# The last features of the second feed-forward product, token by token in the slab scheme's banks

## The chip, the cores and the metric

The kernel runs on one core of one Trainium2 chip. The metric is the device time of one execution in microseconds; 1983.56 us is the median of three runs before the change (1983.42 to 1984.15). Matrix products run on TensorE (PE, its weight loads as PEld), elementwise work on VectorE (DVE) and ScalarE (ACT); GpSimd (POOL) and SyncE (SP) issue transfers.

## What is computed

The reference is a two-layer decoder trunk over 256 tokens of 2048 features, in float32. Layer 0 mixes tokens with a multi-scale causal pooling and a memory cross-attention; layer 1 with a differential attention over shared keys and values and the memory attention. Each layer ends in the same feed-forward block, which is all that matters here:

```python
def squared_relu_mlp(h, w1, w2):
    z = jax.nn.relu(h @ w1)
    return (z * z) @ w2
...
        x = x + squared_relu_mlp(rms_norm(x, ffn_norm[i]), w_ff1[i], w_ff2[i])
```

`w_ff1` is 2048 x 8192 and `w_ff2` 8192 x 2048. The norm's per-token factor is applied after the second product, since relu and the square let it through: as `r[0]` (features by tokens) or `r[1]` (one scalar per token row).

## The kernel before

**Precision.** Every product is made of three matmuls. A 128 x 128 weight block is cast to a high part (ACT, line 195, into `hi_ring`) and a low part is the difference (DVE, line 198, into `lo_ring`); activations are held as high and low too. High times low, high times high and low times high are accumulated in PSUM.

**Feed.** `Feed` streams the weights in the order of use: it loads (SP, `load`), prepares (`_prepare`, `_split`) and hands out blocks. A dry run of the program lists the jobs in order of use; `Plan.close` turns that into the order of preparation. The two rings have `SLOTS = 6` slots of 512 columns. When a job is asked for (`fill`), up to three further entries are prepared if slots are free. Jobs of kind `N` are four blocks for plain use (a quad, one slot); jobs of kind `S` belong to slabs. The casts and low parts of `S` jobs are bound to their order by `feed.order`; the framework's planner orders the rest by its own estimates.

**Slabs.** A slab takes two features (128 rows each of `w_ff2`) and eight blocks of columns for all 256 tokens in the seven products of a Strassen-Winograd scheme instead of eight. Each product has its PSUM bank `banks[0]` to `banks[6]`, which accumulates over slabs. A slab is run in four jobs (lines 943, 945 and 946 are the three matmuls of a product): job 0 uses banks 0 and 1 with plain weights, job 1 bank 2, job 2 banks 3 and 4, job 3 banks 6 and 5 with sums of weights. The sums are made like this, for slab n, with `ra` the first loaded row of blocks and `rb` the second: after job 0's split, POOL adds a part of the second row into `ra` while it is loaded (line 170); the entry `K`, ahead of job 1, adds on DVE (line 224) `ra` and `rb`; job 1 uses the left half of `ra`; job 2 uses `rb`; after job 2's split POOL adds the same part into `rb` (line 170) and DVE adds `ra`'s right half (line 238); job 3 uses `rb`. So

```python
        if p[2] == 0:
            self.add_right(p[1], ra[:, 0:512])
        elif p[2] == 2:
            self.add_right(p[1], rb[:, 512:1024])
            add(rb[:, 0:512], rb[:, 0:512], ra[:, 512:1024])
```

**The feed-forward block (`ffn`).** Of the first product, 8 of 64 output features go through eight slabs, and the other 56 through plain tiles (`up_tile`: 16 blocks each, lines 456 and 458, bank `x_bank`). After each tile its result is added, rectified, squared into `stage`, split into `z` (`convert`) and combined in pairs into sums of activations `sit`. The second product's slabs run between the blocks of the up-tiles: `jobs` is a list of due times (`tiles_at`, in units of up-tiles) in the order (n+1, 0), (n, 1), (n, 2), (n-1, 3). The 2048 outputs are two halves, g = 1 (the left one) and g = 0, which share the seven banks: `slabs` alternates in groups of four, and `swap` copies the banks out (line 1101) and back (line 1093) between them. The left half takes 24 slabs, the right half all 32. When the left half's last slab is done, `close_left` combines its banks, `scale_rows` scales them and `turn_left` transposes them into `resid`.

**The tail.** `last` runs after the 56 up-tiles. Twelve slab jobs are left by then, for the right half. The left half's last 16 features (pairs 24 to 31 hold 16 features; the right half's are done by slabs) are done in eight plain `down_tile`s, one for each of the left half's output blocks, each with 16 blocks; two slab jobs stand ahead of each of the first six. `finish_banks` closes the right half during tile 5. In layer 1 the last tile is made of finer matmuls (`c_tile`, lines 470 to 472), its last four features from `zr`, already scaled. `done(n)` hands a finished output on: to the next layer's operand in layer 0, to the output in layer 1 (line 2049).

Of the kernel before, what the change touches and what calls it, by code (L numbers as in the profile page):

```python
# [17 lines left out]
P = 128  # L18
# [8 lines left out]
PER_PART = 56  # L27
# [28 lines left out]
class Plan:  # L56
# [7 lines left out]
    def __init__(self):  # L64
        self.entries = []
        self.npos = 0
        self.jobs = []
        self.slabs = []

# [31 lines left out]
class Feed:  # L101
# [65 lines left out]
    def add_right(self, n, t):  # L167

        h = self.plan.row["S", n, 1]
        self.nc.gpsimd.dma_start(t, self.wst[h, :, 0:512], accum_op=ALU.add)  # L170
# [40 lines left out]
    def _prepare(self, p):  # L211
# [22 lines left out]
        if p[2] == 0:  # L234
            self.add_right(p[1], ra[:, 0:512])
        elif p[2] == 2:
            self.add_right(p[1], rb[:, 512:1024])
            add(rb[:, 0:512], rb[:, 0:512], ra[:, 512:1024])
# [35 lines left out]

    def used(self, n=1):
# [6 lines left out]
    def slab(self, rows):  # L282

        if self.dry:
            self.plan.slabs.append(rows)
        self.slab_no += 1
# [10 lines left out]
    def job_used(self, n, j):  # L297
        if not self.dry:
            self.free(("S", n, j))

# [11 lines left out]
def program(ctx, tc, plan, dry, xT, memT, par, lam, cst, wst, yT):  # L312
# [129 lines left out]
    def a_part(ps, w, l, n, ks, xs, first=True, last=True, between=None, rows=None):  # L442
# [4 lines left out]
        while i < len(ks):  # L447
# [7 lines left out]
            for c, k, hi, lo in two:  # L455
                nc.tensor.matmul(ps, hi, xs[:, k, :], start=first and c == 0, stop=False)  # L456
# [337 lines left out]
    def ffn(l, xs, tags, done, z, sums_in, f_place):  # L794
# [6 lines left out]

        room = sp.tile([P, 8192], F32, tag=tags[1], name=f"room{l}")
        staged = sp.tile([P, 2048], F32, tag="big2", name=f"stage{l}")
        sit = [sums_in[:, j, :] for j in range(4)]
        stage = [staged[:, T * j : T * j + T] for j in range(6)]
        sums = [room[:, 512 * j : 512 * j + 512] for j in range(2)]
        outs = [room[:, 1024 + 512 * j : 1536 + 512 * j] for j in range(2)]
# [19 lines left out]
        def evict(ps):  # L827
            x = outs[cnt[0] % 2]
            cnt[0] += 1
            return x, nc.scalar.copy(x, ps)  # L830
# [4 lines left out]
        def convert(j):  # L835
            a = stage[j % 6]
            k = j % NK

            def high():
                z_free[k] = False  # L840
                nc.scalar.copy(z[:, k, 0:T], a)
                at(1, low)

            def low():
                nc.vector.tensor_sub(z[:, k, T : 2 * T], a, z[:, k, 0:T].bitcast(F32))
# [3 lines left out]
            if j % 2 == 0:  # L849
                return  # L850
            i = j // 2

            def ready():
                return j in z_done and j - 1 in z_done and sit_free[i % 4]

            def combine():
                summed_up.add(i)
                sit_free[i % 4] = False
                a11, a21 = stage[2 * i % 6][:, 0:P], stage[2 * i % 6][:, P:T]
                a12, a22 = stage[(2 * i + 1) % 6][:, 0:P], stage[(2 * i + 1) % 6][:, P:T]  # L860
                s1, s2, s3, s4 = (sums[i % 2][:, c * P : c * P + P] for c in range(4))
                nc.vector.tensor_sub(s1, a21, a22)
                nc.vector.tensor_sub(s3, a11, a21)
                nc.vector.tensor_sub(s2, s1, a11)
                nc.vector.tensor_add(s4, a12, s2)
                at(1, sums_high)
                at(2, sums_low)

            def sums_high():
                nc.scalar.copy(sit[i % 4][:, 0:512], sums[i % 2])  # L870

            def sums_low():
                nc.vector.tensor_sub(
                    sit[i % 4][:, 512:1024], sums[i % 2], sit[i % 4][:, 0:512].bitcast(F32)
                )
                sit_done.add(i)

            when(ready, combine)

        def up_tile(i, ps, between=None):  # L880
# [5 lines left out]
            y, out = evict(ps)  # L886
            at(1, lambda: nc.vector.tensor_add(y[:, 0:T], y[:, 0:T], y[:, T : 2 * T]))
            at(2, lambda: nc.scalar.activation(y[:, 0:T], y[:, 0:T], AF.Relu))

            def square():  # L890
# [1243 lines left out]
```

## Time and profile before

| | |
|---|---|
| median of the runs | 1983.56 us |
| profiled execution | span 1982.8 us, 31946 instructions |
| TensorE, VectorE, ScalarE, GpSimd busy | 1977.6, 1806.6, 1571.6, 239.3 us |
| layer 0's feed-forward block | first up-tile at 252.2 us, plain down-tiles from 862.2 to 921 us |
| layer 1's | first up-tile at 1310.2 us, plain down-tiles from 1920.5 us to the end |
| transferred | 426.92 MB, mean 215 GB/s |

The page gives busy times of the engines, the span in 40 slices, the queues and the chain of work that ended last. Below it, the trace answers by groups of instructions, by stretches of time (busy microseconds of each engine), by tile or line (durations as min/median/max), and by the timeline (start, duration, engine, line, operation, output <- inputs). Times are from the span's start.

### The profile page before, as it was taken

What the parts mean: (1) busy time and instruction counts of PE and PEld (TensorE: products, weight loads), DVE (VectorE), ACT (ScalarE), POOL (GpSimd) and SP (SyncE); (2) the same over time, 40 slices, a digit from 0 to 9 for tenths busy, and PEclk for the clock granted to TensorE, in tenths of its full rate; (3) what the DMA queues carried; (4) which work ended last, traced back from release to release, by engine and by line L of the source; (5) the groups of instructions that cost most, each with busy time, mean ns of one, the idle gap of its engine ahead of it and who ended that gap; (6) DMA issues with size and microseconds to landing.
All of it is one profiled execution on the core that took longest, in us unless ns stands there. A gap on an engine that the chain in (4) does not pass through costs nothing.

```text
span 1982.8 us, 31946 instructions
## 1 busy us (share of the span) xinstructions
PE 1977.6 (100%) x10356; PEld 1685.5 (85%) x10356; DVE 1806.6 (91%) x3313; ACT 1571.6 (79%) x2886; POOL 239.3 (12%) x281
## 2 busy tenths in 40 slices
PE   9999999999999999999999999999999999999999
PEld 7888888888888888888888889888888888888888
DVE  8898889999999999889989798989999999999888
ACT  7766677788878888778768799777788888888775
POOL 0000011111111111110110000001111111111110
PEclk9999999999999999999999999999999999999999
DMA  9556578888888888767886434568888888988874
GB/s 312 183 183 195 189 207 229 236 232 235 237 233 232 231 233 227 226 182 222 246 222 191 166 127 143 197 188 240 235 231 229 235 234 229 242 231 227 227 207 146
DMA packets 151080, 426.92 MB, mean 215 GB/s; under 512 B 17024, under 2 KB 19712, under 8 KB 150912
## 3 DMA queue, kind: packets, MB, share of 16 engines
q1 hardware_dynamic: 111024, 352.50, 53.2%
q0 software_dynamic: 39744, 72.37, 22.0%
q8 instruction: 81, 1.33, 0.3%
q14 instruction: 87, 0.71, 0.1%
q10 hardware_dynamic: 144, 0.01, 0.0%
HBM read 422.72 MB, written 2.10 MB: 214 GB/s over the span
## 4 chain that ended last, share of the span: by engine, by line
PE 99%; DMA 0%; ACT 0%; SPq 0%; issue 0%; DVE 0%; ACTq 0%
PE x_bank L456 22%; PE x_bank L458 11%; PE p L943 10%; PE p L945 10%; PE p L946 10%; PE wo L456 6%; PE wo L458 3%; PE u L456 2%; PE ff L456 1%; PE u L458 1%; PE q L490 1%; PE q L492 1%; PE q L491 1%; PE mk L492 1%; PE mk L490 1%; PE vp L1642 1%
## 5 line engine op out<-in xcount | busy, mean ns | idle before, releaser
L195 ACT CAST hi_ring<-raw 128x512 fp32r<-128x512 f32 x897 | 547.5, 620 | 167.3 <-PE x_bank L456 39.7
L198 DVE TENSOR_TENSOR lo_ring<-raw,hi_ring 128x512 fp32r<-128x512 f32 x897 | 605.1, 686 | 46.7 <-ACT hi_ring L195 39.9
L456 PE MATMUL x_bank<-fx,hi_ring 128*128 128x512 f32 x1728 | 540.1, 394 | 0.0
L458 PEld LDWEIGHTS x_bank<-fx,lo_ring 128*128 128x128 f32 x1728 | 324.5, 188 | 73.5
L198 DVE TENSOR_TENSOR lo_ring<-room,hi_ring 128x1024 fp32r<-128x1024 f32 x256 | 312.7, 1222 | 44.1 <-ACT hi_ring L195 42.5
L195 ACT CAST hi_ring<-room 128x1024 fp32r<-128x1024 f32 x256 | 269.8, 1054 | 94.4 <-PE x_bank L456 43.2
L458 PE MATMUL x_bank<-fx,lo_ring 128*128 128x256 f32 x1728 | 339.6, 278 | 0.0
L456 PEld LDWEIGHTS x_bank<-fx,hi_ring 128*128 128x128 f32 x1728 | 286.3, 189 | 26.0 <-ACT room L830 1.5
L198 DVE TENSOR_TENSOR lo_ring<-slab,hi_ring 128x1024 fp32r<-128x1024 f32 (+1 forms) x276 | 263.3, 954 | 33.3 <-ACT hi_ring L195 30.2
L195 ACT CAST hi_ring<-slab 128x1024 fp32r<-128x1024 f32 (+1 forms) x276 | 227.7, 834 | 52.5 <-PE p L945 28.2
L170 POOL DMA_DIRECT2D slab<-in_w x138 | 119.6, 866 | 1172.0 <-DVE lo_ring L198 854.0
L943 PE MATMUL p<-hi_ring,sit 128*128 128x512 f32 x480 | 188.3, 392 | 0.0
L945 PE MATMUL p<-hi_ring,sit 128*128 128x512 f32 x480 | 187.4, 390 | 0.0
L946 PE MATMUL p<-lo_ring,sit 128*128 128x512 f32 x480 | 186.6, 389 | 0.0
L170 POOL DMA_DIRECT2D room<-in_w x128 | 110.8, 866 | 486.5 <-DVE lo_ring L198 456.6
L456 PE MATMUL wo<-cat,hi_ring 128*128 128x512 f32 x512 | 161.6, 397 | 0.0
L943 PE MATMUL p<-hi_ring,z 128*128 128x512 f32 x368 | 145.2, 395 | 0.1
L945 PE MATMUL p<-hi_ring,z 128*128 128x512 f32 x368 | 143.9, 391 | 0.0
L946 PE MATMUL p<-lo_ring,z 128*128 128x512 f32 x368 | 143.4, 390 | 0.0
L458 PEld LDWEIGHTS wo<-cat,lo_ring 128*128 128x128 f32 x512 | 95.9, 188 | 22.3
L946 PEld LDWEIGHTS p<-lo_ring,sit 128*128 128x128 f32 x480 | 90.1, 188 | 19.7
L943 PEld LDWEIGHTS p<-hi_ring,sit 128*128 128x128 f32 x480 | 90.0, 187 | 13.1
(495 smaller groups left out, 3610.7 us busy)
## 6 DMA issues: line engine op xcount, KB each, us to landing
raw<-in_w SPq DMA_DIRECT2D x446, 512.0 KB, 4.3
slab<-in_w SPq DMA_DIRECT2D x138, 512.0 KB, 5.7
slab<-in_w POOLq DMA_DIRECT2D x138, 256.0 KB, 5.3
room<-in_w SPq DMA_DIRECT2D x128, 256.0 KB, 4.7
room<-in_w POOLq DMA_DIRECT2D x128, 256.0 KB, 5.5
resid<-in_x SPq DMA_DIRECT2D x8, 256.0 KB, 5.1
kv<-in_mem SPq DMA_DIRECT2D x8, 256.0 KB, 5.3
out_y<-resid SPq DMA_DIRECT2D x16, 128.0 KB, 1.9
```

Source lines behind the costliest of these rows:

```text
L170: self.nc.gpsimd.dma_start(t, self.wst[h, :, 0:512], accum_op=ALU.add)
L195: self.last_cast = self.nc.scalar.copy(hi, src)
L198: low = self.nc.vector.tensor_sub(lo, src, hi.bitcast(F32))
L456: nc.tensor.matmul(ps, hi, xs[:, k, :], start=first and c == 0, stop=False)
L458: nc.tensor.matmul(ps[:, T : 2 * T], lo, xs[:, k, 0:T], start=False, stop=last and c == len(ks) - 1,)
L490: nc.tensor.matmul(ps[t], x[t][1], hi, start=k == 0, stop=False)
L491: nc.tensor.matmul(ps[t], x[t][0], hi, start=False, stop=False)
L492: nc.tensor.matmul(ps[t], x[t][0], lo, start=False, stop=k == NK - 1)
L943: nc.tensor.matmul(ps, a[1], hi, start=new, stop=False, **again)
L945: nc.tensor.matmul(ps, a[0], hi, start=False, stop=False, **again)
L946: nc.tensor.matmul(ps, a[0], lo, start=False, stop=end, **again)
L1642: nc.tensor.matmul(bank, a[0], lo, start=False, stop=end)
```

## The change

Both halves of the second product now go through the same slabs: 29 pairs of features in layer 0 (groups of 4, the last of 1: 58 slabs) and 30 in layer 1 (the last group of 2: 60 slabs). The three or two pairs left (`singles`) are done for both halves token by token: the activations of 128 tokens are the fixed operand and a quad of four weight blocks the moving one, and the result is added into banks 1 and 6 (first column group) or 4 and 2 (second), which hold plain outputs in the scheme (`plain_quad`). In layer 1 the right half's first column group is `held_quad`: all of bank 6 first, then all of bank 1, from the same four held quads.

`down_tile`, `finish_banks` and `zr` go. `last` becomes an explicit list: a quad or a slab job at a time, with layers 0 and 1 different. The right half is closed in steps (`close_right`, `close_c12`, `close_v`, `close_w`, `scaled_sum`, `turn`); its last piece in layer 1 is scaled in two halves, transposed and written out. `turn_left` adds from PSUM directly in layer 0 and through a POOL transfer in layer 1. The two features of a pair change places in the slab; a pair's second feature is split for one half of the tokens only (`Pairs` is the new layout of `z`), sums take three or one DVE operations in place of four, and in layer 1 (`BY_TWO`) two up-tiles are finished together. `far` is never set.

```diff
-PER_PART = 56
+GROUPS = ((4, 4, 4, 4, 4, 4, 4, 1), (4, 4, 4, 4, 4, 4, 4, 2))
+BY_TWO = (False, True)
...
         slabs = []
-        for h in range(6):
-            for g in (0, 1) if h % 2 == 0 else (1, 0):
-                slabs += [(g, 4 * h + i, g == h % 2) for i in range(4)]
-        slabs += [(0, i, False) for i in range(24, 32)]
+        for h, n in enumerate(groups):
+            first = sum(groups[:h])
+            g = (len(groups) - h) % 2
+            slabs += [(g, i, True) for i in range(first, first + n)]
+            slabs += [(1 - g, i, False) for i in range(first, first + n)]
+        n_slabs = len(slabs)
+        w = n_slabs - groups[-1] - 1
+        singles = range(left_pairs, 32)
...
-            return 12.5 + 0.78 * (p - 4) if p <= 47 else 46.04 + 1.6 * (p - 47)
+            if p <= 41:
+                return 12.5 + 0.78 * (p - 4)
+            return 41.36 + 14.2 * (p - 41) / (w - 42)
...
-        for p in range(-9, len(slabs) + 1):
+        for p in range(-9, w - 1):
...
+        def plain_quad(g, c, i, e):
+            hi, lo = feed.quad(weights(g, c, i, e))
+            for p in ((1, 6), (4, 2))[c]:
+                product(p, g, g == 0 and (i, e) == (31, 1), side(p, i, e), hi, lo)
+            feed.used(4)
...
         def last():
+            z_last = n_slabs - 1
+            plain(1, (0, 1), singles[:1])
+            slab((w - 1, 1), (w - 1, 2), (w - 2, 3))
+            if l == 0:
+                plain(1, (0,), singles[1:2])
+                slab((w - 1, 3))
+                plain(1, (1,), singles[1:2])
+                plain(1, (0, 1), singles[2:])
+                slab((w, 0), (w, 1), (w, 2))
+            else:
+                plain(1, (0, 1), singles[1:])
+                slab((w, 0), (w - 1, 3), (w, 1), (w, 2))
+            slab((w + 1, 0), (w, 3), (w + 1, 1), (w + 1, 2))
+            for s in range(w + 2, n_slabs):
+                slab((s, 0), (s - 1, 3), (s, 1), (s, 2))
+            if l == 0:
+                plain(0, (1,), singles[:1])
+                slab((z_last, 3))
+                plain(0, (0,), singles)
+                plain(0, (1,), singles[1:])
+            else:
+                plain(0, (1,), singles)
+                slab((z_last, 3))
+                for p in (6, 1):
+                    tail.extend(("held", p, i, e) for i in singles for e in range(2))
...
+                if x == ("held", 6, 31, 1):
+                    at(1, close_w)
+                if x == ("held", 1, 31, 0):
+                    turn(0, 1, "st")
+                if x == ("held", 1, 31, 1):
+                    for c in range(2):
+                        scaled_sum(1, right["c11"], 0, slice(T * c, T * c + T))
+                    turn(0, 0, "t", (0, 2))
+                    turn(0, 0, "t", (2, 4))
```

In this list `plain(g, cs, which)` stands for one quad for each of the named pairs, column groups and two features, and `slab((s, j), ...)` for job j of slab s. In layer 0 w is 56 and the slabs end at 57; in layer 1 w is 57 and they end at 59.

More of the change, by code (lines that the diff above doesn't have):

```diff
@@ L273, in block, with held, release @@
         return hi[:, s], lo[:, s]
+    def held(self, what):
+        both = self.quad(what)
+        self.pos += 4
+        if self.dry:
+            self.plan.npos = self.pos
+        return both, self.pos // 4 - 1
+    def release(self, n):
+        if not self.dry:
+            self.free(("N", n))
     def used(self, n=1):
@@ L859, in combine @@
[L859 to L866, printed above, removed]
+                summed_up.add(m)
@@ L1055, in close_first @@
             for p in of_job[j]:
-                restore(p, 0)
+                restore(p, slabs[0][0])
         def turn_first(h):
@@ L1271, in ffn @@
         due(56)
-        assert len(jobs) == 12 and not turns
         feed.loads_ahead = LOADS
-        ends = (
-            (2, 0, 0, 0), (2, 0, 0, 0), (2, 0, 0, 0), (2, 0, 0, 0), (2, 0, 0, 0), (2, 0, 0, 0),
-        )
         def last():
-            def some(n):
-                for _ in range(n):
-                    one_job()
-                    tick()
-            def between(n):
-                return lambda b: some(ends[n][b // 4]) if b > 0 and b % 4 == 0 else None
-            for n in range(8):
-                if n < 6:
-                    some(ends[n][0])
-                if n == 5:
-                    finish_banks()
-                ps = bank() if n < 6 else mmt("ff2")
-                down_tile(n, ps, between(n) if n < 6 else None)
+            z_last = n_slabs - 1
@@ new lines, in last, with slab, plain @@
+            tail = []
+            def slab(*what):
+                tail.extend(("slab", s, j) for s, j in what)
+            def plain(g, cs, which):
+                for i in which:
+                    tail.extend(("plain", g, c, i, e) for c in cs for e in range(2))
+            plain(1, (0, 1), singles[:1])
+            slab((w - 1, 1), (w - 1, 2), (w - 2, 3))
+            if l == 0:
+                plain(1, (0,), singles[1:2])
[3 more added lines that the diff above has]
+                slab((w, 0), (w, 1), (w, 2))
+            else:
+                plain(1, (0, 1), singles[1:])
+                slab((w, 0), (w - 1, 3), (w, 1), (w, 2))
@@ new lines, in can, with run @@
+            def can(what, *a):
+                if what == "slab":
+                    return ready(*a)
+                if what == "held":
+                    return holds[a[0]] == 0
+                g, c, i, e = a
+                if any(holds[p] != g for p in ((1, 6), (4, 2))[c]):
+                    return False
+                return i in sit_done if c else 2 * i + e in z_done
+            def run(what, *a):
+                if what == "slab":
+                    jobs[:] = [(0, *a)]
+                    one_job()
+                elif what == "held":
+                    held_quad(*a)
+                else:
+                    plain_quad(*a)
@@ L1296, in ffn @@
+            waited = 0
+            for x in tail:
+                while not can(*x):
+                    tick()
+                    waited += 1
+                    assert waited < 60, (l, x)
+                if turns:
+                    turn_left(turns.pop(0))
+                run(*x)
+                after(*x)
+                tick()
+            assert not turns
         return last
```

334 lines of the change are left out of this document (214 added, 120 removed).

## The prediction

> **What bounds the kernel now.** I read the page first: busy times, slices, and the chain that ended last.
>
> ```profile
> span 1982.8 us, 31946 instructions
> PE 1977.6 (100%) x10356; PEld 1685.5 (85%) x10356; DVE 1806.6 (91%) x3313; ACT 1571.6 (79%) x2886; POOL 239.3 (12%) x281
> PEclk9999999999999999999999999999999999999999
> PE 99%; DMA 0%; ACT 0%; SPq 0%; issue 0%; DVE 0%; ACTq 0%
> ```
>
> TensorE is busy from end to end at full granted clock and makes 99% of the last chain, so less matmul work shortens the run, and any wait that TensorE gains lengthens it one for one. The profiled execution (1982.8 us span) lies 0.8 us under the 1983.56 us median; I sum against the median.
>
> A busy row doesn't show the rate, because matmuls overlap. The timeline's start times do (slab products, then plain blocks of layer 1's tail, then the finer tiles and the transposes near the end):
>
> ```profile
> 1958.07 0.39 PE L945 MATMUL p<-hi_ring,z 128*128 128x512 f32 x1
> ...
> 1960.34 0.39 PE L946 MATMUL p<-lo_ring,sit 128*128 128x512 f32 x1
> 1960.57 0.62 PE L456 MATMUL x_bank<-z,hi_ring 128*128 128x512 f32 x2
> ...
> 1964.74 0.62 PE L456 MATMUL x_bank<-z,hi_ring 128*128 128x512 f32 x2
> ...
> 1973.18 0.28 PE L472 MATMUL ff<-z,lo_ring 128*128 128x256 f32 x1
> ...
> 1975.34 0.28 PE L472 MATMUL ff<-z,lo_ring 128*128 128x256 f32 x1
> ...
> 1975.46 0.27 PE L1185 MATMUL ct<-const,c_b 128*128 128x128 f32 x1
> ...
> 1976.22 0.27 PE L1185 MATMUL ct<-const,c_a 128*128 128x128 f32 x1
> ...
> 1979.08 0.28 PE L472 MATMUL ff<-zr,lo_ring 128*128 128x256 f32 x1
> 1979.39 0.42 DVE L915 TENSOR_TENSOR resid<-resid,ff 128x256 f32<-128x256 f32 x1 [0.55 <-PE ff L472]
> ```
>
> From 1958.07 to 1960.57 eleven 512-column matmuls start: 0.227 us each. So a slab job of two blocks (6 matmuls) is 1.36 us, job 1 (3 matmuls) 0.68, a slab (21) 4.77, and a token-by-token quad (6 matmuls, four blocks) 1.36. From 1960.57 to 1964.74 there are six pairs of plain blocks: 4.17/12 = 0.3475 us a block. In the last output tile six blocks take 2.16: 0.36 each. Eight transposes start 0.11 apart.
>
> **Matmul work removed.** Layer 0's plain part is 8 tiles of 16 blocks: 128 x 0.3475 = 44.5 us. In its place come two slabs (9.55) and 24 quads (3 pairs x 2 features x 2 halves x 2 column groups; 32.7): 42.3, a gain of 2.2. Layer 1 had the same 44.5, plus 16 x 0.0125 = 0.2 for its finer last tile; now four slabs (19.1) and 16 quads (21.8): 40.9, a gain of 3.8. Four of layer 1's last transposes move behind the last product: 0.4 less ahead of it. Together -6.4 us.
>
> **The end of layer 1.** Now the last matmul ends at 1979.36 and the span at 1982.8: 3.4 us, with one 0.42 us DVE operation and the output transfer. Afterwards the chain behind the last product is: two half-width scaled sums (0.42 each, the second overlapping), two transposes, a 0.42 add, then two more transposes, which reuse bank "t" and so wait for that add, a second add, and the transfer. By the rows above: 0.5 + 0.4 + 0.45 + 0.4 + 0.45 before a transfer of 2.95, so 5.1. Cost +1.7 (1.0 if the second pair overlaps, 2.5 if the strided output lands slower).
>
> **Main loops.** They take over two (layer 0) and three (layer 1) slabs from the tails, and two more swaps each of bank copies.
>
> ```profile
> 600.00:700.00 100.00, 100.00 (x509) 84.50 (x508) 93.31 (x146) 87.43 (x148) 18.73 (x22) 1.00 0.88 233
> 860.00:907.80 47.80, 47.80 (x258) 41.08 (x257) 43.75 (x76) 38.10 (x65) 3.46 (x4) 1.00 0.65 189
> L1101 ACT COPY room<-p x46: 570/585/599, 360.2 to 1743.4; 128x512 f32<-128x512 f32 x46
> ```
>
> Columns of the first two rows (busy by stretch): PE, PEld, DVE, ACT, POOL, clock, DMA share, GB/s. A swap is 14 ACT copies of about 0.59: 28 more, 16.5 us a layer, against 12.6 idle of each 100 us. The old schedule's pace is kept to slab 41; later slabs get 0.95 to 1.01 up-tiles where some had 0.78, so VectorE's 93% eases there; the merged sums and the halved conversion of the odd feature take work off it as well. I cost the main loops at nothing; the cover is ACT's and DVE's idle tenth, and without it a bank restore would arrive late. Layer 1's left half returns through a POOL transfer added into `resid`; the output transfers queued on SP behind it are needed by nobody before the end, and eight products follow. Nothing.
>
> **The wait that comes in.** Preparing a slab is a chain. After job 0's cast (ACT) and low part (DVE), POOL issues an accumulating transfer into the block that job 1 and the K sum read; after job 2's low part it issues a second one, into the block that job 3 reads. `feed.order` keeps slab casts and lows in that order. Before, the job order is (n+1,0), (n,1), (n,2), (n-1,3) with plain work between, so each accumulate has about a slab's period:
>
> ```profile
> 864.79 0.86 POOL L170 DMA_DIRECT2D room<-in_w  x1 [6.67 <-DVE lo_ring L198]
> 873.08 0.86 POOL L170 DMA_DIRECT2D slab<-in_w  x1 [7.43 <-DVE lo_ring L198]
> 880.71 0.86 POOL L170 DMA_DIRECT2D room<-in_w  x1 [6.76 <-DVE lo_ring L198]
> ...
> DMA to landing us min/median/max: 3.5/5.4/8.6
> ...
> DMA to landing us min/median/max: 2.6/3.8/5.5
> ```
>
> The last two rows are the landing times of all accumulates (line 170) and of the `room` transfers in layer 0's tail. In the new tails the order is (n,0), (n-1,3), (n,1), (n,2), with no quad between: slabs 56 and 57 of layer 0; 57, 58 and 59 of layer 1. Job 1's accumulate is then issued one preparation before it is needed, and job 3's likewise. The preparations cost:
>
> ```profile
> 866.21 1.22 DVE L198 TENSOR_TENSOR lo_ring<-room,hi_ring 128x1024 fp32r<-128x1024 f32 x1
> 867.34 0.68 DVE L873 TENSOR_TENSOR sit<-room,sit 128x512 fp32r<-128x512 f32 x1
> 867.94 1.29 DVE L198 TENSOR_TENSOR lo_ring<-raw,hi_ring 128x512 fp32r<-128x512 f32 x2
> ...
> L195 ACT CAST hi_ring<-room x7: 1034/1055/1060, 862.2 to 896.9; 128x1024 fp32r<-128x1024 f32 x7
> ```
>
> Start to start a 1024-wide DVE pass is 1.13 us and a 512-wide one 0.60. Follow one cycle, t = 0 when slab n's first accumulate lands. The accumulate for (n-1,3) landed 1.13 earlier; its cast ends at -0.08, its low at 1.05; the K sum ends at 1.65, job 1's low at 2.25, job 2's at 3.4, the next slab's job 0 at 4.6, its accumulate is issued at 4.9 and lands at 4.9 + L. TensorE has 4.77 us of products per slab, so each such cycle shows about L + 0.1. The ring of six slots holds 6 x 0.68 = 4.1 us of products and can hide this once, not per slab. Waits behind it: slab casts queue in order, so products of all later jobs are late too.
>
> Layer 0: the two slots of (56,0) come free as the last four quads start; cast, low and issue 2.6, L, and job 1's cast 0.6, against 4 x 1.36 + 1.36 = 6.8 of products: L - 3.6. Then one cycle, L + 0.1. Then (57,3) waits 0.3 + L + 1.05 against two quads and the rest of job 2, 3.4: L - 2.0. Layer 1: the first accumulate has four quads and two jobs, 8.2: nothing. Then two cycles, 2L + 0.2; (59,3) has four quads ahead: nothing. Together 5L - 5.3.
>
> The landing time L: bounds 3.5 (no accumulate was faster) and 8.6. A slab brings a 512 KB load, a 256 KB load and two 256 KB accumulates (their medians over all loads follow),
>
> ```profile
> slab<-in_w SPq DMA_DIRECT2D x138, 512.0 KB, 5.7
> slab<-in_w POOLq DMA_DIRECT2D x138, 256.0 KB, 5.3
> ```
>
> 1.31 MB in a cycle of over 9 us, some 140 GB/s and below the 189 of the tail's row. So the tail is nearest: 3.8 at the median, 5.5 at most. I take 4.5, a little above that median because the two accumulates now follow each other closely: 17 us; 12 at 3.5, 22 at the overall median 5.4. The adds and bank copies of `close_left` (7 x 0.60 on DVE, 9 x 0.59 on ACT) and job 2's add now stand in the same queues; if they go into the idle spells they cost nothing, if they block casts in program order each layer may lose their 4 to 9 us once. I take +1.
>
> Sum: 1983.56 - 6.4 + 1.7 + 17 + 1 = 1997 us.
>
> [...]
>
> **Rivals.** *Hidden, faster.* The waits don't reach TensorE at all, since preparation runs ahead. For it: no wait of TensorE shows in the tails today, and accumulates are not late anywhere. Against it: the ring's 4.1 us is spent once, and a cycle of 4.9 + L can't fit 4.77. Time: 1983.56 - 6.4 + 1.7 = 1979. It decides at a total wait of 4.7 us: below that the change gains, and below 0.7 it gains over 0.2%. Chance 0.2 (the casts' real order is set by a planner that I see only in its result).
>
> *Half hidden.* Only the full cycles show and L sits near its floor, or the planner finds work for the idle spells: 4 to 10 us of wait, 1983 to 1989. Chance 0.12.
>
> *Queues block.* The in-order casts also wait behind `close_left`'s copies, or L is at its overall median: 24 to 35 us of wait, 2003 to 2014. A cold clock would add to it:
>
> ```profile
> 1981.50:1982.00 0.50, 0.00 (x0) 0.00 (x0) 0.00 (x0) 0.00 (x0) 0.00 (x0) 1.00 0.00 0
> 1982.00:1982.50 0.50, 0.00 (x0) 0.00 (x0) 0.00 (x0) 0.00 (x0) 0.00 (x0) 0.59 0.00 0
> ```
>
> After the last matmul (1979.36) the granted clock falls within 3 us; five idle spells of 3 to 5 us could each be followed by about 3 us at half rate, 1.5 us lost each, 7 in all: 2004. [...] Chance of this rival 0.15.
>
> **How the numbers follow.** The forecast (1990 to 2003) has 0.53. A measurement here tells about 0.2%, 4 us, from no change. Faster (below 1979.6): most of *hidden*, 0.14. Same (to 1987.5): the rest of it and half of *half hidden*, 0.13. Slower 0.73. The range runs from the hidden case, 1979, to the upper part of *queues block*, 2012; the forecast's own range is 1990 to 2003.
>
> **What would show it.** Right: idle TensorE only in the two tails, 7 to 9 us each, ahead of slab products, with ACT casts of `slab` and `room` blocks waiting for DMA; the accumulates of the tails 1 us apart in pairs; last matmul to end 5.1 us; tails of TensorE work 2.2 and 3.8 us shorter when the waits are subtracted. Wrong: no DMA wait on ACT or DVE in the tails (then *hidden*), idle spells in the main loops (bank restores late, DVE short), a clock below 1.00 (cold), or landing times outside 3.5 to 5.5.

## The result and the profile after

The changed kernel is slower: 2004.33 us median of four runs (2003.05 to 2006.27) against 1983.80 (1983.42 to 1984.15) on the same chip, ratio 1.0105 (95% interval 1.0090 to 1.0119). That is inside the range (1979 to 2012), on the predicted side, and 7 us above the predicted 1997, just outside the forecast's own range of 1990 to 2003. The profiled execution is the longest of the four runs (2006.27, span 2004.4; the others' spans are 2001.2 to 2003.5), so its stages hold some 2 us that the median does not.

Span, busy times, the clock in 40 slices and the chain that ended last, from the page after:

```profile
span 2004.4 us, 31465 instructions
PE 1984.2 (99%) x10194; PEld 1674.8 (84%) x10194; DVE 1784.0 (89%) x3133; ACT 1572.1 (78%) x2831; POOL 253.0 (13%) x297
PEclk9999999999999999999999999999999999999999
issue 44%; PE 44%; POOL 9%; DMA 1%; DVE 1%; ACT 1%; POOLq 0%; SPq 0%; ACTq 0%; DVEq 0%
PE wo L496 6%; POOL slab L172 4%; POOL room L172 4%; PE x_bank L496 3%; PE wo L498 3%; PE p L997 2%; PE p L1000 2%; PE p L999 2%; PE u L496 2%; PE x_bank L498 2%; PE u L498 1%; PE q L530 1%; PE q L532 1%; PE q L531 1%; PE mk L530 1%
```

The chain is the first thing to read. Before, TensorE was 99% of it. Now the chain steps back from TensorE through a cast to a transfer and on to POOL's accumulating transfers (line 172, the old line 170): somewhere a wait for them ended last. From there back the chain stays on POOL through most of both main loops; its "issue" (44%) is mostly the time between POOL's transfers there, in which nothing is lost, so the shares of this chain aren't shares of the loss. The busy row does not show it: TensorE is still at 99%, with 162 matmuls fewer in the records and a busy time 6.6 us *longer*: a matmul's recorded duration grows behind a wait (0.50 us at 881.38 below, 0.39 at 879.59) and at half clock (0.63 at 903.15). Start times have to carry the ledger.

The span cut at start times of matmuls ("main" from the first to the last up-tile, "tail" from there to the next block's first key product, or in layer 1 to the last product; "middle" from that key product to layer 1's first up-tile; "end" from the last product's start to the end of the span), in us:

| kernel | start | main 0 | tail 0 | middle | main 1 | tail 1 | end | span |
|---|---|---|---|---|---|---|---|---|
| before | 252.2 | 607.8 | 60.7 | 389.5 | 608.1 | 60.8 | 3.7 | 1982.8 |
| after | 252.1 | 615.5 | 60.7 | 394.6 | 620.0 | 55.5 | 6.0 | 2004.4 |

The main loops take over two and three slabs (9.55 and 14.3) and give up 16 transposes of `turn_left` each (1.8): +7.8 and +12.5 worked out, +7.7 and +11.9 measured, so nothing waits there. A stretch of the main loop (columns as before: PE, PEld, DVE, ACT, POOL, clock, DMA share, GB/s) then some microseconds of the two tails, cut fine:

```profile
600.00:700.00 100.00, 100.00 (x508) 84.58 (x507) 92.73 (x141) 86.85 (x148) 18.60 (x22) 1.00 0.87 231
...
899.00:901.00 2.00, 0.14 (x1) 0.14 (x2) 1.36 (x3) 1.23 (x2) 0.28 (x1) 1.00 0.60 100
...
902.00:903.00 1.00, 1.00 (x3) 0.60 (x3) 0.85 (x3) 1.00 (x3) 0.00 (x0) 0.50 0.00 0
903.00:904.00 1.00, 1.00 (x4) 0.77 (x3) 1.00 (x2) 1.00 (x2) 0.00 (x0) 0.50 0.00 0
904.00:905.00 1.00, 1.00 (x3) 0.50 (x2) 0.77 (x2) 1.00 (x3) 0.00 (x0) 0.50 0.00 0
905.00:906.00 1.00, 1.00 (x6) 0.83 (x5) 1.00 (x2) 1.00 (x3) 0.07 (x1) 1.00 0.00 0
1965.00:1968.00 3.00, 1.01 (x5) 0.35 (x3) 1.77 (x4) 1.94 (x4) 0.86 (x1) 1.00 0.71 113
1968.00:1971.00 3.00, 2.45 (x8) 1.22 (x8) 2.77 (x4) 2.80 (x5) 0.00 (x0) 1.00 0.32 57
1976.00:1978.00 2.00, 0.79 (x5) 0.42 (x4) 0.00 (x0) 0.82 (x2) 1.40 (x2) 1.00 0.82 164
...
1980.00:1982.00 2.00, 2.00 (x8) 1.47 (x7) 1.34 (x2) 1.43 (x2) 0.86 (x1) 0.55 0.78 138
1982.00:1984.00 2.00, 2.00 (x7) 1.62 (x7) 1.73 (x2) 2.00 (x5) 0.21 (x1) 0.60 0.94 222
```

TensorE works 0.14 of 2 us, and then three or four matmuls a microsecond start where it should be 4.4: the granted clock is 0.50 for 3.4 us (901.6 to 905.0). ScalarE's own waits in the first tail (867 to 925 us) and in the second (from 1950 us), each as total, times, longest:

```profile
ACT hi_ring L197 <- DMA room<-in_w: 7.0, 3, 5.1
ACT hi_ring L197 <- DMA slab<-in_w: 5.2, 1, 5.2
...
ACT hi_ring L197 <- DMA slab<-in_w: 4.5, 2, 4.0
...
ACT hi_ring L197 <- DMA room<-in_w: 2.5, 3, 1.2
```

None of these waits for `slab` and `room` existed before. One of them in the timeline: POOL's accumulates, ScalarE's casts, and TensorE behind them (in brackets the idle time before, and what ended it):

```profile
874.44 0.86 POOL L172 DMA_DIRECT2D room<-in_w  x1 [13.42 <-DVE lo_ring L200]
889.00 0.87 POOL L172 DMA_DIRECT2D slab<-in_w  x1 [13.70 <-DVE lo_ring L200]
896.08 0.86 POOL L172 DMA_DIRECT2D room<-in_w  x1 [6.21 <-DVE lo_ring L200]
898.41 0.86 POOL L172 DMA_DIRECT2D slab<-in_w  x1 [1.47 <-DVE lo_ring L200]
...
880.29 1.04 ACT L197 CAST hi_ring<-room 128x1024 fp32r<-128x1024 f32 x1 [5.14 <-DMA room<-in_w]
...
892.69 0.62 ACT L197 CAST hi_ring<-slab 128x512 fp32r<-128x512 f32 x1 [5.24 <-DMA slab<-in_w]
899.77 1.04 ACT L197 CAST hi_ring<-room 128x1024 fp32r<-128x1024 f32 x1 [1.14 <-DMA room<-in_w]
...
879.59 0.39 PE L1000 MATMUL p<-lo_ring,z 128*128 128x512 f32 x1
881.38 0.50 PE L997 MATMUL p<-hi_ring,z 128*128 128x512 f32 x1 [1.40 <-ACT hi_ring L197]
...
900.86 0.50 PE L997 MATMUL p<-hi_ring,z 128*128 128x512 f32 x1 [1.87 <-ACT hi_ring L197]
```

The landing times of line 172's transfers in the two tails:

```profile
DMA to landing us min/median/max: 3.6/3.6/5.7
...
DMA to landing us min/median/max: 3.6/3.9/5.1
```

The accumulate issued at 896.08 lands 3.6 us later at 899.7; the cast starts at 899.77, the product at 900.86. To sum the waits, I take all matmuls that start over 0.26 us behind a 512-column one, and add up what lies beyond 0.227: 11.1 us in tail 0, 9.0 in tail 1, 8.2 in the middle (before: 0.2, 0 and 3.9). In tail 1 a further 1.7 us of idle time, ahead of 1978.39, stands behind a transpose and is not in its sum. The granted clock is 0.50 once in each of the three stages, for 3.4 us each time (901.6 to 905.0, 976.7 to 980.1, 1980.2 to 1983.6; never before the end of the work in the kernel before). Matmuls start 0.43 us apart there, so each of these stretches makes up to 1.7 us of its stage's sum.

### The profile page after: what moved, and what is told of

It reads as the page before. It is cut to its first block, busy times and chain, and to the rows that moved or that the text cites. A ratio compares the mean times of both kernels' runs of the same rounds, so it can differ in the third digit from the quotient of the medians.

```text
span 2004.4 us, 31465 instructions
## 1 busy us (share of the span) xinstructions
PE 1984.2 (99%) x10194; PEld 1674.8 (84%) x10194; DVE 1784.0 (89%) x3133; ACT 1572.1 (78%) x2831; POOL 253.0 (13%) x297
## 4 chain that ended last, share of the span: by engine, by line
issue 44%; PE 44%; POOL 9%; DMA 1%; DVE 1%; ACT 1%; POOLq 0%; SPq 0%; ACTq 0%; DVEq 0%
PE wo L496 6%; POOL slab L172 4%; POOL room L172 4%; PE x_bank L496 3%; PE wo L498 3%; PE p L997 2%; PE p L1000 2%; PE p L999 2%; PE u L496 2%; PE x_bank L498 2%; PE u L498 1%; PE q L530 1%; PE q L532 1%; PE q L531 1%; PE mk L530 1%
## 5 line engine op out<-in xcount | busy, mean ns | idle before, releaser
L197 ACT CAST hi_ring<-raw 128x512 fp32r<-128x512 f32 x873 | 532.7, 620 | 155.1 <-PE wo L496 38.4
L200 DVE TENSOR_TENSOR lo_ring<-raw,hi_ring 128x512 fp32r<-128x512 f32 x873 | 588.3, 685 | 45.5 <-ACT hi_ring L197 40.7
L200 DVE TENSOR_TENSOR lo_ring<-room,hi_ring 128x1024 fp32r<-128x1024 f32 x268 | 327.3, 1222 | 74.1 <-ACT hi_ring L197 70.2
L197 ACT CAST hi_ring<-room 128x1024 fp32r<-128x1024 f32 x268 | 282.1, 1053 | 123.8 <-PE p L999 49.1
L200 DVE TENSOR_TENSOR lo_ring<-slab,hi_ring 128x1024 fp32r<-128x1024 f32 (+1 forms) x288 | 274.6, 953 | 36.4 <-ACT hi_ring L197 32.7
L197 ACT CAST hi_ring<-slab 128x1024 fp32r<-128x1024 f32 (+1 forms) x288 | 237.6, 834 | 66.9 <-PE p L999 31.1
L997 PE MATMUL p<-hi_ring,sit 128*128 128x512 f32 x524 | 207.3, 396 | 0.8 <-ACT hi_ring L197 0.7
L1000 PE MATMUL p<-lo_ring,sit 128*128 128x512 f32 x524 | 204.8, 392 | 1.5 <-DVE lo_ring L200 1.5
L999 PE MATMUL p<-hi_ring,sit 128*128 128x512 f32 x524 | 205.5, 392 | 0.0
L997 PE MATMUL p<-hi_ring,z 128*128 128x512 f32 x446 | 176.5, 396 | 7.2 <-ACT hi_ring L197 7.1
L1000 PE MATMUL p<-lo_ring,z 128*128 128x512 f32 x446 | 174.8, 393 | 1.1 <-DVE lo_ring L200 1.0
L999 PE MATMUL p<-hi_ring,z 128*128 128x512 f32 x446 | 174.4, 391 | 0.0
```

What stands on the lines that cost most here:

```text
L197: self.last_cast = self.nc.scalar.copy(hi, src)
L200: low = self.nc.vector.tensor_sub(lo, src, hi.bitcast(F32))
L997: nc.tensor.matmul(ps, a[1], hi, start=new, stop=False, **again)
L999: nc.tensor.matmul(ps, a[0], hi, start=False, stop=False, **again)
L1000: nc.tensor.matmul(ps, a[0], lo, start=False, stop=end, **again)
```

## The experiments

Before's median beside each group was 1983.2 to 1983.8. A kernel's stages are listed in the table at the end of this section.

**The sums left out.** `e1_no_accum`: no accumulating transfer for a slab from w - 1 on; the two sums of weights that they make are left out.

```diff
+        alone = p[1] in self.plan.far          # far: slabs s >= w - 1
-        if p[2] == 0:
+        if p[2] == 0 and not alone:
             self.add_block(p[1], 1, 0, ra[:, 0:512])
         elif p[2] == 2:
-            self.add_block(p[1], 1, 0, rb[:, 512:1024])
+            if not alone:
+                self.add_block(p[1], 1, 0, rb[:, 512:1024])
...
```

> The changed kernel without the two accumulating transfers of the tails' slabs (55 to 57 in layer 0, 56 to 59 in layer 1): their sums of weights are left out, every other instruction stays. Landing theory (TensorE waits in the tails for accumulates issued one preparation before use): nearly all of the tails' idle time goes, 1982 to 1988 us; what stays is the end of layer 1 (+2) and the slower stretch between the feed-forward blocks (+5). Queue theory (the copies and adds that close the left half, and slabs that follow each other faster than VectorE can split them, hold up the casts): the landing was hidden behind these, at most a third goes, 1997 us or more.

Measured 1989.87 (1989.35 to 1990.67), ratio 1.0032 (1.0021 to 1.0044): 14.5 us less than the changed kernel, 7.3 in each tail. The chain that ended last, of this kernel's page:

```profile
PE 96%; DVE 2%; DMA 1%; ACT 1%; issue 0%; SPq 0%; ACTq 0%; DVEq 0%
```

POOL is gone from it. The accumulates carry most of the loss. The run stays 2 us above the upper end that the landing theory gave; 6.9 us of waits remain in the tails (2.8 and 4.2), with no accumulate in them. The granted clock never falls to 0.50 in this profile's tails (its mean over the run is 1.0), so up to 3.4 of the 14.5 us were half clock that followed the waits.

**Order alone, and three other suspects.** `e2_spread` only reorders the tails' list so that quads stand between an accumulate and its reader; `e3_sit_free` lets layer 0's bank 4 quads read `z` in place of the sums (another product than the reference's), so that a buffer comes free earlier for the next layer; `e4_no_close` cuts the copies, adds, restores and scalings of `close_left` to two columns (the left half's result is left out).

```diff
 # e2, layer 1 (layer 0 alike)
-                plain(1, (0, 1), singles[1:])
-                slab((w, 0), (w - 1, 3), (w, 1), (w, 2))
-            slab((w + 1, 0), (w, 3), (w + 1, 1), (w + 1, 2))
+                plain(1, (0,), singles[1:])
+                slab((w, 0))
+                plain(1, (1,), singles[1:])
+                slab((w - 1, 3), (w + 1, 0), (w, 1), (w, 2))
+                slab((w + 2, 0), (w + 1, 1), (w + 1, 2))
...
 # e3
-            if p == 4:
+            if p == 4 and (g or l):
...
 # e4
-                nc.scalar.copy(left["u"], banks[0])
-                add(left["c11"], left["u"], banks[1])
+                nc.scalar.copy(left["u"][:, 0:2], banks[0][:, 0:2])
+                add(left["c11"][:, 0:2], left["u"][:, 0:2], banks[1][:, 0:2])
```

> The changed kernel with its tail lists in another order: the same slab jobs and quads, but between a slab's job 0 and job 1, and between its job 2 and job 3, stand at least three other jobs or quads. Landing theory: the landings pass under products, 1983 to 1990 us. Queue theory: the same work stands in the same queues, 1998 to 2005 us.

> The changed kernel with bank 4's quads of layer 0's right half reading z in place of the sums of activations (those products are then of other data), so that the sums' buffer is free some 10 us before the tail ends. Buffer theory (the memory rows that layer 1 loads into this buffer come late, and ACT waits for them in the next stage with the casts queued behind): the stretch between the feed-forward blocks is about 4 to 5 us shorter, 1998 to 2001 us. Rival (that stretch is slower because layer 0's last features are handed on later): no change, 2003 to 2006 us.

> The changed kernel with the copies, adds, restores and scalings that close the left half cut to 2 of 512 columns (the left half's result is then left out), all waits between them kept. Landing theory: the queues lose some 10 us of work a layer, but it stood in idle spells: 2000 to 2005 us. Queue theory: the tails lose most of their idle time, 1994 us or less.

`e2_spread`: 1997.32 (1993.87 to 1998.92), between the two theories: tails 6.1 and 5.2 us shorter, but its end grew to 8.7 us: the left half is closed later, its last POOL transfers into `resid` start at 1977.9 to 1982.7, and seven output transfers are then issued on SP from 1987.2 on. `e3_sit_free`: 2005.16 (2003.18 to 2005.77), no gain: the first three loads of the memory rows moved from -0.5 to -15.6 us relative to the key product, the other five stayed; the buffer theory of the middle stretch falls. `e4_no_close`: 2001.86 (2000.16 to 2003.70), 2.5 us less, 1.5 of it in the tails of the profiled runs: what `close_left` puts into the queues is a minor term.

**The same sums without the transfers.** If the landing is what costs, the sums made on VectorE from blocks that are already on chip must do nearly as well as no sums. `e7_sums_dve` and `e9_sums_after` load the tails' second rows whole and add there; in e7 the sum of all three blocks is written over job 1's block ahead of its cast, so job 1 multiplies by another sum than the reference's; e9 has it behind the cast and computes everything.

```diff
+        src, n = (
+            (ra, 2),
+            (ra[:, 0:512], 1),
+            ((ra[:, 0:512], rb[:, 512:1024]), 2),
+            ((ra[:, 512:1024], rb[:, 0:512]), 2),
+        )[p[2]]
...
+        if p[2] == 0:
+            add(ra[:, 0:512], ra[:, 0:512], rb[:, 0:512])
+        elif p[2] == 1:
+            add(ra[:, 0:512], ra[:, 0:512], rb[:, 512:1024])
+        elif p[2] == 2:
+            add(ra[:, 512:1024], ra[:, 512:1024], ra[:, 0:512])
+            add(rb[:, 0:512], rb[:, 0:512], rb[:, 512:1024])
```

> Changed kernel with the same numbers computed; for the last three slabs of layer 0 and the last four of layer 1 the second row is loaded whole and the sums of weights are made by VectorE from blocks already on chip (two more 128x512 adds a slab, job 2 and 3 cast in two pieces), so no accumulating transfer is issued for them. Landing theory (the tails' waits are the accumulates' landing times): as with the accumulates left out, 1989.9 us, plus what VectorE pays: a slab then needs about 6.5 us of it against 4.8 us of products, up to 1.7 us for each of five slabs without a quad beside them: 1990 to 1997 us, tails of about 54 to 57 and 49 to 53 us against 60.7 and 55.5. Rival (the tails wait for the in-order queues of casts and lows, which this loads more): 2002 us or more.

> The same as e7_sums_dve, with the two further sums moved behind job 1's cast and low part and job 2's, so that neither the block of job 1 is overwritten (in e7 job 1 read the sum of all three blocks) nor job 1's cast waits for them; all numbers of the reference are computed. Landing theory: with no accumulate in the tails they stand between those of the kernel without sums (53.4 and 48.2 us) and those of e7 (54.1 and 52.4): 1990 to 1996 us. Rival (in-order queues of casts and lows, now loaded by about 6.5 us of VectorE a slab against 4.8 us of products): 1997 us or more.

e7: 1996.32 (1995.00 to 1996.54). e9: 1994.48 (1992.75 to 1997.17), ratio 1.0055 (1.0042 to 1.0069). Both in the landing theory's interval: with all the work done and VectorE loaded more, 9.9 us come back.

**The middle stretch.** It grew by 5.1 us and the prediction had nothing there. ScalarE's largest waits for the memory rows in it, after and before:

```profile
ACT mems L472 <- DMA kv<-in_mem: 4.7, 3, 2.8
```

```profile
ACT mems L433 <- DMA kv<-in_mem: 2.7, 3, 1.4
```

and the splits of the first features for layer 1 in layer 0's tail, after (the first key product is at 928.3) and before (920.8):

```profile
914.33 0.91 ACT L472 ACTIVATE x_kv<-resid,param 128x256 fp32r<-128x256 f32 x2 [0.30 <-DVE resid L1224]
...
920.87 0.91 ACT L472 ACTIVATE x_kv<-resid,param 128x256 fp32r<-128x256 f32 x2
```

```profile
871.48 0.51 ACT L433 ACTIVATE x_kv<-resid,param 128x256 fp32r<-128x256 f32 x1
...
911.59 0.51 ACT L433 ACTIVATE x_kv<-resid,param 128x256 fp32r<-128x256 f32 x1
```

The left half is now finished in the tail, so features 0 to 7 are split from 14 us ahead of the key product on; before, it was one every 8 us, from 49 us ahead. `e5_mem_loads` leaves out the last five loads of memory rows (their splits read older rows); `e6_features` splits features 0 to 7 early in the tail, without the left half's part; `e12_after_deferred` only sets ten of the memory rows' splits later.

```diff
 # e5
-    for p in range(8):
-        at(5 * p + 3 if p >= 3 else 4 + p // 2, lambda p=p: mem_again(p))
+    for p in range(3):
+        at(4 + p // 2, lambda p=p: mem_again(p))
...
 # e6, in last(), in place of the two calls in turn_left
+            if l == 0:
+                for c in range(8):
+                    at(3 + 2 * c, lambda c=c: done(c))
...
 # e12 (the loads p = 6 and 7 three steps later as well)
-        at(12 + 9 * k // 4, lambda k=k: mem_split(k))
+        at(min(49, 20 + 9 * k // 4) if k > 5 else 12 + 9 * k // 4, lambda k=k: mem_split(k))
```

> Left out of the changed kernel: the last five of the eight loads of the second layer's memory rows (kv<-in_mem, p from 3), so their splits read rows that are there already. In the changed kernel the stretch between layer 0's tail and layer 1's first up-tile is 394.6 us against 389.5 before; ScalarE waits 2.8 us for such a load at 970.7 us with casts behind it, and TensorE stalls 2.0 us just then. Theory 'late loads': these loads are issued 9 to 16 us later (relative to the first key product) than before, and hold the in-order cast queue; without them that stretch is 390 to 392 us and the run 2000 to 2002 us. Rival 'late features': the normalized features 0 to 7 are split only at the end of layer 0's tail and push the whole of ScalarE's and VectorE's work back; then the stretch stays at 393.5 us or more and the run at 2003 to 2005 us.

> Changed kernel, but in layer 0 the features 0 to 7 are split for layer 1 (x_kv, and their later sums) from the third step of the tail on, one every two steps, instead of after turn_left has added to them; they so lack the left half's contribution. Theory 'late features': the 5 us by which the stretch between the layers grew come from these splits and the sums behind them lying in the last 14 us of the tail, where they stood 49 to 9 us ahead before; with them back in place the stretch is 390 to 392 us, and layer 0's tail is unchanged or up to 1 us longer; the run 2000 to 2002 us. Rival 'late loads': the stretch stays at 393.5 us or more, the run at 2003 to 2005.

> The changed kernel with only the later splits of e11. Full computation. Theory 'held casts': the middle stretch 390 to 392 us against 394.6, everything else as in the changed kernel, the run 2000 to 2002.5 us. Rival 'late features': 393 us or more, 2003 to 2005 us.

e5: 2003.70 (2002.24 to 2004.34), middle 390.4. e6: 2002.22 (2001.58 to 2002.82), middle 391.0. e12: 2003.55 (2002.41 to 2005.97), middle 392.0, its last ten splits at 28.5 to 45.4 us behind the key product where the changed kernel has 29.2 to 44.7, so it did not do what it was meant to. Kernels whose middle code is that of the changed one have 391.7 to 395.0, so e12 shows nothing, and e5 and e6 stand a little below all of them. The changed kernel's own 394.6 holds the stretch of half clock from 976.7 on, up to 1.7 us, which no other profile has here; e1, e3, e7, e8, e9 and e12 have 392.0 to 392.9, and that is the fairer comparison. The runs as wholes fell by only 0.6 and 2.1 us; e5's tail 0 came out 1.5 longer, with two stretches of half clock in place of one. What orders all the profiles is when the features are split. First split before the key product, and the middle: 49 and 59 us ahead, 389.5 and 391.0 (before, e6); 16 us, 391.7 (e4); about 14 us, 392.0 to 394.6 (seven kernels with the loads in); 8.6 to 10.8 us, 395.0 to 398.0 (e2, and e10 and e11 below, where 0.9 of it are eight transposes that the other kernels have in the tail). In e6 the fourth load of memory rows also left at +6.1 us in place of +21.6. That order fits late features as a cause, but these kernels differ in other ways too; only e6 moves the splits alone, and gains 1 to 2 us on its like; e5, without the loads, gains about 2. How much is held by the loads and how much by the splits and sums is not settled.

**The end.** `e8_end_direct` adds layer 1's left half on VectorE straight from the bank and puts the last pair of transposes into bank "o".

```diff
-            x = outs[h % len(outs)]
-            nc.scalar.copy(x, t4.rearrange("p c t -> p (c t)"))
-            nc.gpsimd.dma_start(to, x, accum_op=ALU.add)
+            nc.vector.tensor_add(resid[:, c : c + 2, :], resid[:, c : c + 2, :], t4)
...
-                    turn(0, 0, "t", (2, 4))
+                    turn(0, 0, "o", (2, 4))
```

> Changed kernel; in layer 1 the left half is added into resid by VectorE straight from the bank, as in layer 0, in place of a copy and a POOL transfer, and the very last pair of transposes goes to another bank so that it need not wait for the add before it. Theory of the end (each term as the trace shows): the second pair's wait of 0.5 us goes, last product to end 5.5 in place of 6.0 us; nothing else moves, the run 2003 to 2004.5 us. Rival: the POOL transfers into resid and the ScalarE copies hold up the tail's accumulates and casts; then layer 1's tail shortens by 1.5 us or more as well and the run is 2002.5 us or less.

2007.68 (2007.20 to 2008.19): slower than the changed kernel by 3.3, a miss for both. The end is 5.6 against 6.0, as the theory had it, but tail 1 grew from 55.5 to 57.3: four adds of 0.6 each (start to start) now stand in VectorE's queue between the low parts. That they are the cause is not shown; half clock also lasts 6.8 us in this tail, against 3.4, but it does so in e3 and e12 too, whose tail 1 has 55.2. (Tail 0, whose code is unchanged, is 2.1 longer in this profile, with two stretches of half clock against one.)

**All of it together.** `e10_together`: e9, the last five memory loads issued from POOL's queue, quads between the last slabs, bank "o". `e11_deferred`: the same with the loads back on SP and e12's later splits.

```diff
 # layer 1's tail in e10 and e11 (layer 0 alike); a, z = singles[0], singles[-1]
+                slab((w - 1, 3), (w, 1), (w, 2), (w + 1, 0), (w, 3))
+                one(1, a, 0)
+                slab((w + 1, 1), (w + 1, 2))
+                one(1, a, 1)
+                slab((w + 2, 0), (w + 1, 3))
+                one(1, z, 0)
+                slab((w + 2, 1), (w + 2, 2))
+                one(1, z, 1)
+                slab((w + 2, 3))
```

> e9's sums on VectorE; the last five in_mem loads issued from POOL's queue in place of SP's; in both tails the token-by-token quads set between the last slabs (left half's close no later); the last pair of transposes in another bank. Full computation. Landing theory: a quad takes 1.36 us of TensorE and 0.69 of VectorE, so six quads between slabs give back some 4 us of what VectorE lacked in e9, tails of 51 to 53 and 47 to 50 us; late-loads theory: the loads leave POOL's empty queue as soon as their tiles are free, the stretch between the layers 390 to 392 us; end 5.5. Together 1981 to 1988 us. Rival (loads were late because the features' splits were, not because of SP's queue): the stretch stays at 392 us or more and the run at 1986 to 1992.

> e10 with all in_mem loads back on SP's queue, and the splits of the memory rows from feature 6 on set 8 steps later (the last four at step 49, ahead of the first use of their tiles; their readers come 80 us later). Full computation. Theory 'held casts' (the middle stretch is long because these splits wait on ScalarE for late loads, with the weight casts queued behind them): the stretch falls from e10's 398.0 and e9's 392.5 to 390 to 391.5 us, the run to 1983 to 1986 us, about the time before. Rival 'late features' (the splits and sums of features 0 to 7 themselves, run at the end of the tail, leave ScalarE and VectorE behind): 392.5 us or more, the run 1987 or more.

e10: 1992.02 (1990.82 to 1992.73), ratio 1.0042 (1.0028 to 1.0055). e11: 1989.98 (1989.27 to 1991.40), ratio 1.0034 (1.0021 to 1.0048). The tails are as short as foreseen or shorter, 51.7 and 46.5. A stretch of the first tail, in the changed kernel and in e10, and e10's longest waits of TensorE:

```profile
862.00:912.00 50.00, 44.50 (x185) 32.42 (x183) 35.15 (x53) 31.89 (x54) 4.32 (x5) 0.97 0.54 152
```

```profile
862.00:912.00 50.00, 48.77 (x223) 38.96 (x222) 44.54 (x76) 38.65 (x73) 0.00 (x0) 1.00 0.47 163
```

```profile
PE vp L1867 <- DVE lo_ring L204: 2.4, 4, 1.1
PE p L1029 <- DVE lo_ring L204: 2.1, 4, 0.7
PE vp L1865 <- ACT hi_ring L201: 1.6, 3, 0.9
```

TensorE gets 38 more matmuls into the same 50 us. Its longest waits are now in the middle stretch (`vp`), which grew to 398.0 in e10 and 395.6 in e11. Another queue for the loads did not help (rival of e10): they left POOL's queue 24 to 45 us behind the key product, later than SP's in the changed kernel (22 to 39). e11's stretch is 2.4 shorter than e10's, not down to the 391.5 of its theory; its later splits began at 30.4 us behind the key product, as in e10 (31.0), and none was more than 4 us later, so it hardly tests that theory. Features are split later still in this order. The end did not shorten either (6.0 and 6.5). Neither kernel beats the kernel before.

| kernel | main 0 | tail 0 | middle | main 1 | tail 1 | end | span |
|---|---|---|---|---|---|---|---|
| e1 no sums | 615.5 | 53.4 | 392.2 | 620.1 | 48.2 | 6.3 | 1987.4 |
| e2 order | 615.7 | 54.6 | 395.0 | 620.1 | 50.3 | 8.7 | 1995.9 |
| e3 buffer | 615.5 | 62.6 | 392.9 | 620.1 | 55.2 | 6.0 | 2003.7 |
| e4 close_left | 615.6 | 59.3 | 391.7 | 620.1 | 55.4 | 6.0 | 1999.8 |
| e5 memory loads | 615.5 | 62.2 | 390.4 | 620.1 | 55.5 | 5.8 | 2001.1 |
| e6 features | 615.4 | 61.0 | 391.0 | 620.2 | 55.3 | 6.0 | 2000.5 |
| e7 VectorE sums | 616.1 | 54.1 | 392.9 | 620.4 | 52.4 | 6.3 | 1993.2 |
| e8 end | 615.6 | 62.8 | 392.7 | 620.1 | 57.3 | 5.6 | 2005.3 |
| e9 VectorE sums | 616.1 | 55.0 | 392.5 | 620.1 | 50.9 | 6.3 | 1992.4 |
| e10 together | 616.2 | 51.7 | 398.0 | 620.1 | 46.5 | 6.0 | 1989.8 |
| e11 deferred | 616.5 | 51.5 | 395.6 | 620.6 | 46.5 | 6.5 | 1988.1 |
| e12 later splits | 615.6 | 61.1 | 392.0 | 620.0 | 55.2 | 6.0 | 2001.5 |

## Why the prediction was right, and where its terms were off

Profiled span against profiled span the loss is 21.6 us; the prediction's sum was 13.3. The median, 2004.33, lies in the interval of *queues block* (2003 to 2014), to which the prediction gave 0.15, and not in its forecast's. Term by term:

- **Matmul work, -6.4 predicted, -5.7 to -7.4 measured** (main and tail of both layers, less the sums above: 665.1 against 668.4, and 666.5 against 668.8; the lower value takes off the 1.7 us ahead of 1978.39 as well). Reading a rate from start times, not from busy time, held.
- **Main loops, nothing: right.** They grew by their slabs and by no wait.
- **The wait for accumulates, 17 predicted: right in mechanism, its parts off in both directions.** The landing time taken was 4.5; the tails' accumulates land in 3.6 to 3.9 at the median. With 3.7 the formula 5L - 5.3 gives 13.2. What disappears with the accumulates (e1) is 14.6 us of the tails, and the sums account for it: they fall from 11.1 and 9.0 to 2.8 and 4.2, and the 1.7 us ahead of 1978.39 go. Two parts of it are not in the formula. Layer 0's (55,3) has no term, but stands only two quads behind (54,3): its accumulate (874.44, landing 5.75) ended a stall of 1.6 us at 881.38. And half clock, which the prediction had only in a rival, at five spells of 3 to 5 us, came after spells of 2.0 us (900.86) and 1.7 us (1978.39), 3.4 us each time, and took up to 3.4 us together. Without these, at least 9.6 us are left for the places that the formula counts, where it gives 13.2; that the total came near is luck in part. The rival's 3 us at half rate behind each spell, 7 us in all, was the author's estimate and is shown by no run: the kernel before has 0.50 only from 1982.1 us to the end of its span at 1982.8; the changed kernel has it for 3.4 us (901.6 to 905.0), up to 1.7 us lost each time.
- **Queues, 1 predicted: too little.** With no accumulate in the tails 6.9 us of waits remain (0.2 before), for casts and low parts. `close_left` is the smaller part of it: 2.5 us for the whole run. Setting quads between slabs, with sums on VectorE, brings the tails' waits to 6.2 from e9's 12.8 (which hold up to 1.7 of half clock); TensorE's products of a slab (4.77) leave little beside what a slab asks of VectorE and ScalarE.
- **The middle stretch: the step that failed.** Nothing was costed between the feed-forward blocks; it is 5.1 us in this profile, up to 1.7 of them half clock, and 2.2 to 5.5 over the kernels with its code. The prediction followed `close_left` into the tail as copies and adds in two queues; that `turn_left` goes with it, and hands the features that the next layer begins with over some 35 us later, it did not see. That this is the cause is likely by e6 and not settled against the late loads.
- **The end, +1.7 predicted, +2.3 measured.** The rows of the last 6 us:

```profile
1998.41 0.40 PE L1000 MATMUL p<-lo_ring,z 128*128 128x512 f32 x1
1998.85 0.87 DVE L388 SCALAR_TENSOR_TENSOR room<-p,d_x,room 128x256 f32<-128x256 f32 x2
...
1999.39 0.44 PE L1258 MATMUL ct<-const,room 128*128 128x128 f32 x2 [0.57 <-DVE room L388]
1999.86 0.42 DVE L1260 TENSOR_TENSOR resid<-resid,ct 128x256 f32<-128x256 f32 x1
...
2000.34 0.44 PE L1258 MATMUL ct<-const,room 128*128 128x128 f32 x2 [0.51 <-DVE resid L1260]
2000.81 0.42 DVE L1260 TENSOR_TENSOR resid<-resid,ct 128x256 f32<-128x256 f32 x1 [0.53 <-PE ct L1258]
```

The chain is the one described, transposes waiting for the add included: from the last product's modelled end (1998.81) its steps take 2.4 us where the terms gave 2.2, and the transfer 3.2 where it was 2.95.

Of the signs named, these came: idle spells in the tails alone among the feed-forward stages, casts of `slab` and `room` blocks waiting for transfers, untouched main loops. These did not: the accumulates of a pair are 2.3 us apart, not 1, since the next job's cast and low part stand between them; the clock was not 1.00 (its mean was 0.997); one landing (5.75) was outside 3.5 to 5.5; and the saving of 2.2 and 3.8 us shows only over main loop and tail together (3.3, and 2.3 to 4.1), not in the tails, because the slabs moved between them. *Hidden* and *half hidden* fall with e1 (14.5 us); *queues block* described the size of the total, but by terms that e4 shows to be small.

## What to carry to other kernels

Where a buffer is loaded by an accumulating transfer, the order of jobs is a timetable: count the products between its issue and its reader, and when a reorder shortens that below the landing time (3.6 to 3.9 us at the median in the tails here), expect up to the difference at each recurrence. Here the summands were on chip already, and adds of 0.6 us on VectorE did better than transfers that land after 3.6 (e9: 9.9 us back). Moving the finish of one half to the end also moves what the next stage reads first; price that hand-over at the next stage's first waits, not in the stage that is edited.

The matmul work saved in this kernel, whose feeders were 79 and 91% busy before (ScalarE, VectorE), was less than the slack that its order held: in the best version here (e11) main loop and tail together are 0.5 and 1.7 us shorter than before, of 6.4 us saved; the stretch between the layers is 6.1 and the end 2.8 us longer, and the run 6.5.

## What the hardware showed that was not expected

Half clock after short spells: idle spells of 2.0 and 1.7 us (ahead of 900.86 and 1978.39) were each followed by 3.4 us at a granted clock of 0.50, while one of 1.9 us (ahead of 1967.95) was not: the rows from 1965 to 1971 have the clock at 1.00. The stall at 881.38 (1.6 us) was not followed by half clock in the changed kernel, where the rows from 880 to 900 have 1.00, but the same stall was followed by it in e3, e5 and e8 (tail 0 62.6, 62.2 and 62.8 us against 60.7). The edges of these stretches in the changed kernel:

```profile
901.50:901.60 0.10, 0.10 (x2) 0.10 (x1) 0.10 (x1) 0.10 (x1) 0.00 (x0) 0.94 0.16 21
976.60:976.70 0.10, 0.10 (x2) 0.06 (x2) 0.10 (x2) 0.10 (x2) 0.10 (x1) 0.90 0.00 0
1980.10:1980.20 0.10, 0.10 (x2) 0.03 (x1) 0.00 (x0) 0.00 (x0) 0.02 (x1) 0.99 1.45 266
1980.20:1980.30 0.10, 0.10 (x2) 0.07 (x1) 0.00 (x0) 0.00 (x0) 0.10 (x1) 0.50 0.78 143
```

The clock falls at 901.59, 976.68 and 1980.20 us: 0.73 us behind the start of the product at 900.86, 1.85 us behind that at 974.83, with a spell of 1.3 us ahead of it and one of 0.7 us behind it (ahead of 976.09), and 1.81 us behind that at 1978.39. Tails 0 with the same code have one stretch of half clock (the changed kernel, e12) or two (e5, e8). Which spells the clock falls after, and when, is not shown: no run changes these spells alone.

Accumulates landed faster in the tails: 3.6 to 3.9 us at the median in stretches that move 127 to 152 GB/s, against 5.4 over all of them in either kernel, most of which stand in main loops at some 230 GB/s.
